# adaLN's sums over partitions on VectorE instead of on TensorE and ScalarE

## The chip, the cores and the metric

The kernel runs on one core of one Trainium2 chip. The metric is the device time of one execution in microseconds (us). The engines are called TensorE (PE in the profile, its weight loads PEld), VectorE (DVE), ScalarE (ACT), GpSimd (POOL) and SyncE (SP, which issues the DMAs).

## The reference

One layer of a conditioned short-convolution mixer on a sequence of 256 positions, all in float32, with D = 2048 and E = 4096:

```python
def rmsnorm(x, g):
    y = xf * lax.rsqrt(jnp.mean(xf * xf, axis=-1, keepdims=True) + EPS)
    return (y * g.astype(jnp.float32)).astype(x.dtype)

def adaln(h, c, w, b):                       # w: (D, 3 D)
    mod = jnp.einsum('bd,df->bf', jax.nn.silu(c), w) + b
    shift, scale, gate = jnp.split(mod, 3, axis=-1)
    h = h * (1.0 + scale[:, None, :]) + shift[:, None, :]
    return h, gate

def short_conv_mixer(h, w_in, conv_w, w_out):
    b_gate, c_gate, v, g = jnp.split(jnp.einsum('bsd,de->bse', h, w_in), 4, axis=-1)
    u = causal_depthwise_conv(c_gate * v, conv_w)
    y = b_gate * u * jax.nn.silu(g)
    return jnp.einsum('bse,ed->bsd', y, w_out)

h, gate = adaln(rmsnorm(x, norm_g), c, ada_w, ada_b)
x = x + gate[:, None, :] * short_conv_mixer(h, sc_w_in, sc_conv_w, sc_w_out)
return rmsnorm(x, final_g)
```

What matters here is `mod`: a vector-matrix product over D = 2048 rows of `ada_w`. Its first 4096 columns give shift and scale, without which `h`, and so the large product with `w_in`, cannot be formed.

## The kernel before, in words

**Products.** Each float32 operand is split into a high part (a cast, `hi`, on ScalarE) and a low part (`lo`, a subtraction on VectorE); a product is three matmuls, hi x hi, hi x lo and lo x hi (`product`, L515). `h` stands transposed as `hT`, 16 k tiles of 128 features; k tile k holds its high part in columns 0 to 255 (written by ScalarE, L361) and its low part behind it (VectorE, L362 and L363).

**The first half of the product with `w_in`** runs while `ada_w` is still being loaded. Output is cut into chunks of 512 columns (chunks 0 to 3, of each of the four quarters c, v, g, b) and each chunk fills one PSUM bank pair (a "bank" below; three of them are used in turn, `mm_s`). The features become ready in eight groups of two k tiles; group 0 (k tiles 0 and 1) is summed in another way before the loop, groups 2, 4, ..., 14 (named by their first k tile) in it. So each (pair of chunks, quarter) is done in several passes over the k tiles that are ready; `plan()` makes the list of 30 passes before anything is emitted. A pass over two chunks with two k tiles is one *block* of 48 matmuls; a longer pass has several. There are 65 blocks, counted from 0. The order is fixed ahead, and each engine executes its instructions in the order in which the program emits them (`in_order`), as long as not all features are ready.

When a pass ends, its banks are closed (`close_bank`, `keep`): in the first pass over an output the bank is copied to SBUF (`acc`, ScalarE, L551). A later pass either adds its bank to `acc` on VectorE (L553), or is *seeded*: ScalarE copies `acc` into the bank before the pass (`open_bank`, L690), the matmuls add to it, and ScalarE copies it out again (L551). `plan()` chooses between the two for each bank by comparing its estimated clocks of ScalarE and VectorE.

**One group of adaLN sums.** Partition p holds the 16 rows p, 128 + p, 256 + p, ... of `ada_w`, so a group's sum over D is a weighted sum over 16 slices, which VectorE makes in 8 pieces of two instructions of 128x512 (`ada_sums`, L495 for the first slice, L497 for the others; columns: shift and scale, two k tiles of 128 each), and a sum over the 128 partitions. For the latter `ada_turn` (L504) has TensorE transpose the four 128x128 parts into a PSUM tile `tp_g`, and `ada_total` (L511) has ScalarE run over each with a copy that accumulates, which gives `gs`, one column of 128 for each part. `all_scales` (L656 to L658, VectorE, three instructions) adds the biases and multiplies by the norm's weight; `all_features` (L361 on ScalarE, L362 and L363 on VectorE, once for each k tile) makes `hT`.

**The emission loop** (L740 to L796) walks through the blocks and keeps a clock for each engine with estimated durations (`SUM_US`, `HI_US`, `TOTAL_US` and so on) to decide what goes where. For block b it emits: the closing of the last pass's second bank; the high part of block b+2; pieces of adaLN sums that end before that high part does (`sum_some`); the low part of block b+2; what is missing of the features that this block needs (`get_ready`); seeds of the next pass; more pieces; the products of the first chunk. Between the products of its two chunks stand the transposes of a group whose pieces ended at least `TURN_US` before that point on the planner's TensorE clock (`turn_sums`), the closing of the pass's first bank and the opening of the next one's second, the totals (`total_sums`), the scales, the features, and again pieces that fit. A piece's DMA is issued when an earlier piece is summed (four are held), the weights of block b+3 when the low part of block b is made.

**Behind this stage** (from about 380 us) the rest of `w_in` (`mm_b`) and `w_out` (`mm_o`) follow; the change doesn't touch them.

Of the kernel before, what the change touches and what calls it, by code (L numbers as in the profile page):

```python
# [8 lines left out]
F32 = mybir.dt.float32  # L9
F32R = mybir.dt.float32r  # L10
AF = mybir.ActivationFunctionType
ALU = mybir.AluOpType

P = 128
# [36 lines left out]
RAW0 = 22.9  # L51
FIRST = 24.0
ISSUE_US = 2.0
TURN_US = 1.0
EARLY_US = 2.0
CONV_AT = 44
LOAD_US = 2.65
# [4 lines left out]
SUM_US = 1.5  # L62
STALL_US = 0.4
AHEAD_US = 3.0
ADD_US = 1.22
COPY_US = 1.03
TOTAL_US = 1.9
FEATURE_US = 0.5


# [4 lines left out]
def plan():  # L75
    steps, ready = [], [0.0] * ADA[0]
    done = {}
    pieces = [(sum(ADA[:g]), nk, i) for g, nk in enumerate(ADA) if g for i in range(4 * nk)]
    load, pe, dve, act = 0.0, 4.0, 0.0, 0.0
    burst = SLOT // P  # L80
    credit = 0.0

    def ada():
        nonlocal load, dve
        piece = pieces.pop(0)
        load = max(load, dve - AAHEAD) + ALOAD
        dve = max(dve, load + 2.0) + VPIECE
        if piece[2] == 4 * piece[1] - 1:
            ready.extend([dve + ALAG] * piece[1])
        return piece  # L90

    def products(n, need):

        nonlocal load, pe, dve, act, credit
        between = []
        load = max(load, pe - WAHEAD)
        pe = max(pe, need, load + min(n, burst) * LOAD + WLAG) + n * PRODUCTS
        for s0 in range(0, n, burst):
            sn = min(burst, n - s0)
            load += sn * LOAD  # L100
            act = max(act, load + 2.0) + sn * SBLOCK
            dve = max(dve, load + 2.0) + sn * VBLOCK
            credit += SHARE * sn / burst
            between.append([])
            while pieces and credit >= 1.0:
                credit -= 1.0
                between[-1].append(ada())
        return between

    order = [((ch, ch + 1), q) for ch in range(0, NCH, 2) for q in QUARTERS]  # L110
    new = [((0,), QUARTERS[0]), ((1,), QUARTERS[0])] + order[1:]
    while new or any(k < KT for k in done.values()):
        before = []
        hi = sum(r <= pe for r in ready)
        if new:
            p = new.pop(0)
            k0 = done[p] = 0
            if p not in order:
                del done[p]
                done[order[0]] = hi  # L120
        else:
            old = [p for p in order if done[p] < KT]
            p = old[0] if hi == KT else min(old, key=lambda p: done[p])
            k0 = done[p]
            while hi == k0:
                while len(ready) == hi:
                    before.append(ada())
                    credit -= 1.0
                pe = max(pe, ready[hi])
                hi = sum(r <= pe for r in ready)  # L130
        between = products((hi - k0) * CT * len(p[0]), ready[hi - 1])
        hows = []
        for _ in p[0]:
            seed = k0 > 0 and act < dve
            if k0 == 0:
                act += SCOPY
            elif seed:
                act += SSEED
            else:
                dve += VSUM  # L140
            hows.append(seed)
        steps.append((before, *p, k0, hi, hows, between))
        if p in order:
            done[p] = hi
    blocks = [b for step in steps for b in step[-1]][: len(PACE)]
    some = [piece for b in blocks for piece in b]
    for b, n in zip(blocks, PACE):
        b[:], some = some[:n], some[n:]
    blocks[-1].extend(some)
    return steps  # L150
# [3 lines left out]
def short_conv_layer(ctx: ExitStack, tc: tile.TileContext, x, c, norm_g, ada_w, ada_b, w_in, conv_w, w_out, final_g, out):  # L154
    nc = tc.nc
# [6 lines left out]
    const = ctx.enter_context(tc.tile_pool(name="const", bufs=1))  # L162
# [3 lines left out]
    psum = ctx.enter_context(tc.tile_pool(name="psum", bufs=3, space=PSUM))  # L166
# [58 lines left out]
    pinned.enter_context(in_order())  # L225


    rows1 = const.tile([80, P], F32, tag="rows1", name="rows1")
    rows2 = const.tile([96, P], F32, tag="rows2", name="rows2")
    HX = D // 2  # L230
    GIVE = 300
# [12 lines left out]
    for n in range(KT // 4):  # L244
        at = wpool.tile([P, SLOT], F32, tag=("lo", "hi")[n % 2], name="at0", bufs=3)
# [50 lines left out]
    b_shift = vec[:, 16:32]  # L296
    b_scale1 = vec[:, 32:48]
    b_both = vec[:, 16:48].rearrange("p (s k) -> p s k", s=2)
    sh_sc = const.tile([P, KT // 2, 2], F32, tag="shsc", name="sh_sc")
    idle(1, turned[2])  # L300
    idle(2, turned[2])
# [194 lines left out]
            else:  # L496
                nc.vector.scalar_tensor_tensor(out=gv, in0=at4[:, i], scalar=c_k, in1=gv, op0=ALU.mult, op1=ALU.add)  # L497

    def ada_turn(k0, nk):

        tp = psum.tile([P, 4, P], F32, tag="sm", name="tp_g", bufs=2)
        gv = sums[k0][:, :, 0 : nk * P]
        for o in range(2 * nk):
            nc.tensor.transpose(tp[:, o, :], gv[:, o // nk, (o % nk) * P : (o % nk + 1) * P], ident)  # L504
        return tp

    def ada_total(nk, tp):

        gs = const.tile([P, 4], F32, tag="gs", name="gs", bufs=2)
        for o in range(2 * nk):  # L510
            nc.scalar.activation(tp[:, o, :], tp[:, o, :], AF.Copy, accum_out=gs[:, o : o + 1])  # L511
        return gs[:, 0:nk], gs[:, nk : 2 * nk]

    opener = [None]
    def product(dst, hi, lo, k, i, begins, left, ends):  # L515
# [45 lines left out]
    N = len(flat)  # L561
    todo = [item for b, block in enumerate(flat) for item in [("w", b)] + [("a", p) for p in block[-1]]][1:]
    raws, parted = {}, {0: (hi0, lo0)}
    waiting, turning, totals, whole_sums, scaled = [], [], [], [], []
    banks = {}
    clock = dict(dma=RAW0, pe=FIRST, dve=RAW0 - ISSUE_US, act=FIRST)
    ready = [NK0]
# [4 lines left out]
    def spend(engine, us, since=0.0):  # L572

        clock[engine] = max(clock[engine], since) + us
        return clock[engine]
# [47 lines left out]
    def sum_one():  # L623

        (k0, nk, piece), at4, at = waiting.pop(0)
        ada_sums(k0, nk, piece, at4)
        spend("dve", SUM_US, at)
        if piece == 4 * nk - 1:
            turning.append((k0, nk, clock["dve"]))
        issue()  # L630

    def sum_some(end, stall):

        while waiting and waiting[0][2] <= clock["dve"] + stall and max(clock["dve"], waiting[0][2]) + SUM_US <= end:
            sum_one()

    def turn_sums(by):

        while turning and turning[0][2] <= by:
            k0, nk, _ = turning.pop(0)  # L640
            totals.append((k0, nk, ada_turn(k0, nk)))

    def total_sums():

        while totals:
            k0, nk, tp = totals.pop(0)
            whole_sums.append((k0, nk, ada_total(nk, tp), spend("act", TOTAL_US, clock["pe"])))

    def all_scales():

        while whole_sums:
            k0, nk, (sums_shift, sums_scale), at = whole_sums.pop(0)
            while waiting and max(clock["dve"], waiting[0][2]) + SUM_US <= at + STALL_US:
                sum_one()
            ks = slice(k0, k0 + nk)
            nc.vector.tensor_tensor(out=scale[:, ks], in0=sums_scale, in1=b_scale1[:, ks], op=ALU.add)  # L656
            nc.vector.tensor_tensor(out=scale[:, ks], in0=scale[:, ks], in1=gT[:, ks], op=ALU.mult)
            nc.vector.tensor_tensor(out=shift[:, ks], in0=sums_shift, in1=b_shift[:, ks], op=ALU.add)  # L658
            spend("dve", STALL_US, at)
            scaled.append((k0, nk))  # L660

    def all_features():
# [9 lines left out]
    def get_ready(k):  # L672

        while ready[0] < k:
            while not turning and not totals and not whole_sums and not scaled:
                issue()
                sum_one()
            turn_sums(clock["dve"])
            total_sums()
            all_scales()  # L680
            all_features()
# [58 lines left out]
    for b, (n, chs, q, k0, k1, seeds, w, s0, sk, _) in enumerate(flat):  # L740
# [20 lines left out]
                open_bank(n + 1, 1)  # L761
        adds = last and len(chs) == 2 and k0 > 0 and not seeds[0]
        sum_some(begin + us / len(chs), STALL_US)
        hi, lo = parted.pop(b)
        parted[b] = None
        for j in range(len(chs)):
            bank = banks[n, j]
            if b == 0:
                for k in range(NK0):
                    chunk_products(bank, hi, lo, k * w, k, k0, k1, late=True)  # L770
            elif k0 == 0 and b + j < 4:
                opening_products(bank, hi, lo, w, j * CT * P, s0, sk, k1)
            else:
                for i in range(sk):
                    chunk_products(bank, hi, lo, i * w + j * CT * P, s0 + i, k0, k1, seeds[j])
            if j == 0:
                clock["pe"] = begin + us / len(chs)
                turn_sums(clock["pe"] - TURN_US)
                if last and len(chs) == 2:
                    close_bank(n, 0)  # L780
                    if n + 1 in passes:
                        open_bank(n + 1, 1)
                total_sums()
                all_scales()
                all_features()
                sum_some(end + AHEAD_US, STALL_US)
                mix_some(end + AHEAD_US)
# [232 lines left out]
```

## Time and profile before

| | |
|---|---|
| Time, median of 3 runs | 913.02 us (911.69 to 913.05) |
| The profiled execution's own time | 911.95 us |
| Its span, first to last instruction | 910.2 us |
| Mean granted TensorE clock | 0.998 |
| TensorE busy | 897.1 us (99%) |
| VectorE busy | 633.5 us (70%) |
| ScalarE busy | 453.1 us (50%) |
| Blocks 0 to 64 (`mm_s`) | about 24 to 379 us |
| Transposes of the sums (L504) | 28, from 61.2 to 239.7 us |
| Their totals on ScalarE (L511) | 28, from 62.8 to 241.2 us |

A page and several views were read. In the groups of instructions a row is "line engine operation out<-in shapes xcount | busy us, mean ns | idle us before them <-what ended it". In the timeline a row is "start us, us, engine line operation out<-in shapes xcount [idle before <-what ended it]"; instructions of one kind that follow each other are merged. In the chain of waits a row is "start us, us, what": the piece of work that the end of the program waited for at that time. The waits view has "who <- for whom: us in total, times, longest us". In the table of windows each engine has its busy us and its count of instructions, then the granted clock, the share of the DMA engines and GB/s. VectorE's and ScalarE's instructions overlap a little at their ends, so the time from one start to the next is often 0.07 to 0.1 us shorter than the duration.

### The profile page before, as it was taken

The numbers are of one execution on the slowest core, as the hardware profiler recorded it, in microseconds if no ns is written. First come the engines' busy times: TensorE is split into PE (matmuls) and PEld (weight loads), VectorE is DVE, ScalarE is ACT, GpSimd is POOL, SyncE is SP. The second block draws the span as 40 slices with busy tenths as digits, with TensorE's granted clock in tenths as the row PEclk, the third lists the DMA queues.
The fourth block names the chain that finished last, engine by engine and source line by source line (L and its number), as shares of the span: only waits on it lengthen the run. The fifth ranks groups of instructions, "written<-read, shape, count | busy, mean of one in ns | idle before, by whom it ended". The sixth has DMA issues, their size and how long they took to land.

```text
span 910.2 us, 16162 instructions
## 1 busy us (share of the span) xinstructions
PE 897.1 (99%) x7045; PEld 859.1 (94%) x7045; DVE 633.5 (70%) x603; ACT 453.1 (50%) x430; POOL 1.8 (0%) x8
## 2 busy tenths in 40 slices
PE   7999999999999999999999999999999999999996
PEld 4999999999999999999999999999999988888885
DVE  5788889999656868776666666656666644555882
ACT  6788766455545746543344443344333433433333
POOL 0000000000000000000000000000000000000000
PEclk9999999999999999999999999999999999999999
DMA  9999999999565555797687778777877496665542
GB/s 310 379 382 364 313 339 347 324 325 354 198 206 190 186 190 201 246 304 240 211 262 245 237 223 269 242 237 230 256 241 240 143 358 205 201 204 188 186 139 92
DMA packets 146855, 227.63 MB, mean 250 GB/s; under 512 B 5456, under 2 KB 103904, under 8 KB 146400
## 3 DMA queue, kind: packets, MB, share of 16 engines
q1 hardware_dynamic: 146688, 226.56, 74.4%
q8 instruction: 55, 0.90, 0.4%
q14 instruction: 16, 0.13, 0.0%
q0 software_dynamic: 64, 0.02, 0.0%
q10 hardware_dynamic: 32, 0.01, 0.0%
HBM read 224.48 MB, written 2.10 MB: 249 GB/s over the span
## 4 chain that ended last, share of the span: by engine, by line
PE 95%; DMA 3%; ACT 1%; DVE 1%; SPq 0%; issue 0%; ACTq 0%
PE mm_b L519 38%; PE mm_s L519 37%; PE mm_o L917 6%; PE mm_o L918 6%; PE mm_o L916 6%; DMA at<-in_ada_w_dram 2%; DMA raw_s<-in_sc_w_in_dram 1%; DMA raw<-in_sc_w_in_dram 0%; PE tp_g L504 0%; ACT hi L611 0%; PE ps_gate L854 0%; SPq L236 0%; ACT tp_g L511 0%; DVE lo L444 0%; DVE lo L618 0%
## 5 line engine op out<-in xcount | busy, mean ns | idle before, releaser
L519 PE MATMUL mm_b<-hT,hi 128*128 128x256 f32 x2048 | 348.4, 276 | 0.0
L519 PE MATMUL mm_s<-hT,hi 128*128 128x256 f32 x2048 | 347.2, 277 | 0.7 <-DVE hT L363 0.5
L519 PEld LDWEIGHTS mm_b<-hT,hi 128*128 128x128 f32 x2048 | 308.6, 188 | 0.1
L519 PEld LDWEIGHTS mm_s<-hT,hi 128*128 128x128 f32 x2048 | 306.5, 188 | 1.5 <-DVE hT L363 0.7
L519 PE MATMUL mm_b<-hT,lo 128*128 128x256 f32 x1024 | 282.6, 276 | 0.0
L519 PE MATMUL mm_s<-hT,lo 128*128 128x256 f32 x1024 | 277.5, 276 | 0.2 <-DVE lo L618 0.2
L370 DVE TENSOR_TENSOR lo<-raw,hi 128x2048 fp32r<-128x2048 f32 x64 | 146.7, 2292 | 114.9 <-ACT hi L369 114.9
L369 ACT CAST hi<-raw 128x2048 fp32r<-128x2048 f32 x64 | 122.5, 1913 | 197.7 <-PE mm_b L519 142.5
L519 PEld LDWEIGHTS mm_b<-hT,lo 128*128 128x128 f32 x1024 | 192.2, 188 | 0.0
L519 PEld LDWEIGHTS mm_s<-hT,lo 128*128 128x128 f32 x1024 | 189.8, 188 | 0.4 <-DVE lo L618 0.4
L618 DVE TENSOR_TENSOR lo<-raw_s,hi 128x2048 fp32r<-128x2048 f32 (+1 forms) x64 | 145.5, 2273 | 49.1 <-ACT hi L611 47.7
L611 ACT CAST hi<-raw_s 128x2048 fp32r<-128x2048 f32 (+1 forms) x64 | 121.5, 1898 | 105.1 <-PE mm_s L519 82.7
L370 DVE TENSOR_TENSOR lo<-raw_o,hi 128x2048 fp32r<-128x2048 f32 x32 | 73.3, 2290 | 63.6 <-ACT hi L369 63.4
L369 ACT CAST hi<-raw_o 128x2048 fp32r<-128x2048 f32 x32 | 61.0, 1907 | 106.4 <-PE mm_o L918 84.5
L917 PE MATMUL mm_o<-lo,y 128*128 128x512 f32 x256 | 99.3, 389 | 0.0
L918 PE MATMUL mm_o<-hi,y 128*128 128x512 f32 x256 | 99.3, 389 | 0.0
L916 PE MATMUL mm_o<-hi,y 128*128 128x512 f32 x256 | 99.3, 389 | 0.0
L497 DVE SCALAR_TENSOR_TENSOR gv<-at,silu_c,gv 128x512 f32<-128x512 f32 x105 | 78.7, 750 | 2.7
L916 PEld LDWEIGHTS mm_o<-hi,y 128*128 128x128 f32 x256 | 48.1, 188 | 10.0
L917 PEld LDWEIGHTS mm_o<-lo,y 128*128 128x128 f32 x256 | 48.0, 188 | 10.0
L918 PEld LDWEIGHTS mm_o<-hi,y 128*128 128x128 f32 x256 | 48.0, 188 | 9.9
L551 ACT COPY acc<-mm_s 128x1024 f32<-128x1024 f32 x43 | 43.2, 1013 | 9.0 <-PE mm_s L519 8.7
(106 smaller groups left out, 377.6 us busy)
## 6 DMA issues: line engine op xcount, KB each, us to landing
raw<-in_sc_w_in_dram SPq DMA_DIRECT2D x64, 1024.0 KB, 6.7
raw_s<-in_sc_w_in_dram SPq DMA_DIRECT2D x63, 1024.0 KB, 6.0
raw_o<-in_sc_w_out_dram SPq DMA_DIRECT2D x32, 1024.0 KB, 5.2
at<-in_ada_w_dram SPq DMA_DIRECT2D x126, 256.0 KB, 6.7
at_g<-in_ada_w_dram SPq DMA_DIRECT2D x32, 512.0 KB, 7.5
x<-in_x_dram SPq DMA_DIRECT2D x4, 512.0 KB, 6.3
big<-in_x_dram SPq DMA_DIRECT2D x2, 1024.0 KB, 7.6
out_dram<-big SPq DMA_DIRECT2D x4, 512.0 KB, 2.9
```

Source lines behind the costliest of these rows:

```text
L369: nc.scalar.copy(hi[:, :n], raw[:, :n])
L370: last_low[0] = nc.vector.tensor_tensor(out=lo[:, :n], in0=raw[:, :n], in1=hi[:, :n].bitcast(F32), op=ALU.subtract)
L497: nc.vector.scalar_tensor_tensor(out=gv, in0=at4[:, i], scalar=c_k, in1=gv, op0=ALU.mult, op1=ALU.add)
L519: mm = last_mm[0] = nc.tensor.matmul(dst, w, h[:, k], start=begins and left, stop=ends, skip_group_check=True)
L551: nc.scalar.copy(acc[ch, q], bank)
L611: nc.scalar.copy(hi[:, :n], raws[b][:, :n])
L618: nc.vector.tensor_tensor(out=lo[:, :n], in0=raws.pop(b)[:, :n], in1=hi[:, :n].bitcast(F32), op=ALU.subtract)
L916: nc.tensor.matmul(po, yh, hi[:, o], start=opens, stop=False, skip_group_check=True)
L917: nc.tensor.matmul(po, yh, lo[:, o], start=False, stop=False, skip_group_check=True)
L918: nc.tensor.matmul(po, yl, hi[:, o], start=False, stop=ct == NCT - 1, skip_group_check=True)
```

## The change

The sum over partitions of a group moves to VectorE. The 128x512 tile of a group is transposed in blocks of 32x32 into a PSUM tile, so that what lay in 32 partitions of one column lies in 32 neighbouring columns of one partition; a sum over those 32 columns leaves 16 columns (`by_block`, 128x16); four copies bring the four groups of 32 partitions next to each other in 32 partitions (`side`); and four small sums over the four groups write `gs`, one for each 32 partitions of the result. Both small tiles lie in columns of `rows1`, a tile whose rows were used up at the start. The transposes on TensorE and the accumulations on ScalarE are gone, and with them `turn_sums`.

The emission changes with it. The totals are emitted in two places: in `get_ready`, and in each block ahead of its first products, behind the low part and the pieces. They wait for no point of the TensorE clock. They spend 2.1 us on the planner's VectorE clock (before: 1.9 on ScalarE's). `all_scales` no longer emits pieces ahead of the scales. In `plan()`, every bank of a later pass over more than two k tiles is seeded, whatever the clocks say.

```diff
-TURN_US = 1.0
...
-TOTAL_US = 1.9
+TOTAL_US = 2.1
...
-            seed = k0 > 0 and act < dve
+            seed = k0 > 0 and (act < dve or hi - k0 > 2)
...
-    rows1 = const.tile([80, P], F32, tag="rows1", name="rows1")
+    rows1 = const.tile([P, P], F32, tag="rows1", name="rows1")
...
+    by_block = rows1[:, 0:16]
+    side = rows1[0:32, 16:80].rearrange("p (g b) -> p g b", g=4)
...
-    def ada_turn(k0, nk):
-
-        tp = psum.tile([P, 4, P], F32, tag="sm", name="tp_g", bufs=2)
-        gv = sums[k0][:, :, 0 : nk * P]
-        for o in range(2 * nk):
-            nc.tensor.transpose(tp[:, o, :], gv[:, o // nk, (o % nk) * P : (o % nk + 1) * P], ident)
-        return tp
-
-    def ada_total(nk, tp):
-
-        gs = const.tile([P, 4], F32, tag="gs", name="gs", bufs=2)
-        for o in range(2 * nk):
-            nc.scalar.activation(tp[:, o, :], tp[:, o, :], AF.Copy, accum_out=gs[:, o : o + 1])
-        return gs[:, 0:nk], gs[:, nk : 2 * nk]
+    def ada_total(k0, nk):
+
+        tp = psum.tile([P, 512], F32, tag="sm", name="tp_g", bufs=2)
+        nc.vector.transpose(tp, sums[k0].rearrange("p s f -> p (s f)"))
+        nc.vector.reduce_sum(by_block, tp.rearrange("p (b j) -> p b j", j=32), axis=mybir.AxisListType.X)
+        for g in range(4):
+            nc.vector.tensor_copy(out=side[:, g, :], in_=by_block[32 * g : 32 * g + 32, :])
+        gs = const.tile([P, 2, nk], F32, tag="gs", name="gs", bufs=2)
+        for g in range(4):
+            nc.vector.reduce_sum(
+                gs[32 * g : 32 * g + 32], side.rearrange("p g (s k b) -> p b s k g", s=2, k=nk)[:, g], axis=mybir.AxisListType.X
+            )
+        return gs[:, 0], gs[:, 1]
...
     def total_sums():
 
-        while totals:
-            k0, nk, tp = totals.pop(0)
-            whole_sums.append((k0, nk, ada_total(nk, tp), spend("act", TOTAL_US, clock["pe"])))
+        while turning:
+            k0, nk = turning.pop(0)
+            whole_sums.append((k0, nk, ada_total(k0, nk)))
+            spend("dve", TOTAL_US)
 
     def all_scales():
 
         while whole_sums:
-            k0, nk, (sums_shift, sums_scale), at = whole_sums.pop(0)
-            while waiting and max(clock["dve"], waiting[0][2]) + SUM_US <= at + STALL_US:
-                sum_one()
+            k0, nk, (sums_shift, sums_scale) = whole_sums.pop(0)
...
-            spend("dve", STALL_US, at)
+            spend("dve", STALL_US)
...
         sum_some(begin + us / len(chs), STALL_US)
+        total_sums()
         hi, lo = parted.pop(b)
...
                 clock["pe"] = begin + us / len(chs)
-                turn_sums(clock["pe"] - TURN_US)
                 if last and len(chs) == 2:
                     close_bank(n, 0)
                     if n + 1 in passes:
                         open_bank(n + 1, 1)
-                total_sums()
                 all_scales()
                 all_features()
```

More of the change, by code (lines that the diff above doesn't have):

```diff
@@ L563, in short_conv_layer @@
     raws, parted = {}, {0: (hi0, lo0)}
-    waiting, turning, totals, whole_sums, scaled = [], [], [], [], []
+    waiting, turning, whole_sums, scaled = [], [], [], []
     banks = {}
@@ L628, in sum_one @@
         if piece == 4 * nk - 1:
-            turning.append((k0, nk, clock["dve"]))
+            turning.append((k0, nk))
         issue()
@@ L635, in sum_some @@
             sum_one()
[L637 to L641, printed above, removed]
     def total_sums():
-        while totals:
-            k0, nk, tp = totals.pop(0)
-            whole_sums.append((k0, nk, ada_total(nk, tp), spend("act", TOTAL_US, clock["pe"])))
+        while turning:
+            k0, nk = turning.pop(0)
+            whole_sums.append((k0, nk, ada_total(k0, nk)))
+            spend("dve", TOTAL_US)
     def all_scales():
         while whole_sums:
-            k0, nk, (sums_shift, sums_scale), at = whole_sums.pop(0)
-            while waiting and max(clock["dve"], waiting[0][2]) + SUM_US <= at + STALL_US:
-                sum_one()
+            k0, nk, (sums_shift, sums_scale) = whole_sums.pop(0)
             ks = slice(k0, k0 + nk)
@@ L674, in get_ready @@
         while ready[0] < k:
-            while not turning and not totals and not whole_sums and not scaled:
+            while not turning and not whole_sums and not scaled:
                 issue()
                 sum_one()
-            turn_sums(clock["dve"])
             total_sums()
```

## The prediction, made before the result was known

> **What bounds the kernel now.** I read the page first: the busy shares and the chain that ended last.
>
> ```profile
> span 910.2 us, 16162 instructions
> PE 897.1 (99%) x7045; PEld 859.1 (94%) x7045; DVE 633.5 (70%) x603; ACT 453.1 (50%) x430; POOL 1.8 (0%) x8
> PE 95%; DMA 3%; ACT 1%; DVE 1%; SPq 0%; issue 0%; ACTq 0%
> ```
>
> TensorE (PE) is the bound: 95% of the chain is its own work. So two things alone can move the end: work that leaves or joins TensorE's queue, and waits that TensorE gains or loses. VectorE (DVE) and ScalarE (ACT) count only where TensorE would wait for them. The waits view says where it waits for the adaLN features now, and the chain in order of time shows that place.
>
> ```profile
> PEld mm_s L519 <- DVE hT L363: 0.7, 1, 0.7
> ...
> 61.43 0.44 PE tp_g L504 x4
> 61.86 32.70 PE mm_s L519 x288
> 94.56 0.45 PE tp_g L504 x4
> ...
> 97.09 0.61 ACT hT L361
> ...
> 98.18 0.44 DVE hT L363
> 98.61 0.04 issue
> 98.66 6.43 PE mm_s L519 x54
> ...
> 239.55 0.44 PE tp_g L504 x4
> ```
>
> There is one such wait in the program, of 0.7 us as the view counts it: block 14 begins, needs the features of k tile 4, and gets them at 98.6. A row below gives it at the matmuls: one starts at 97.75, the next at 98.66, against 32.70 / 288 = 0.1135 us from one to the next elsewhere, so 0.8 us were lost. The seven groups of transposes (L504, the first at 61.43, the last at 239.55) lie on the chain with 0.44 to 0.45 us each.
>
> The stage in which all this happens, 39 to 241 us, has a busy VectorE: 202.00 - 180.57 = 21 us of idle time.
>
> ```profile
> 39.00:241.00 202.00, 201.28 (x1767) 200.81 (x1767) 180.57 (x194) 134.84 (x155) 0.00 (x0) 1.00 0.96 336
> ```
>
> **The change, part by part. What TensorE loses.** Seven times four transposes.
>
> ```profile
> 61.27 0.60 PE L504 MATMUL tp_g<-ident,gv 128*128 128x128 f32 x4
> 61.62 0.48 PE L519 MATMUL mm_s<-hT,hi 128*128 128x256 f32 x2
> 97.75 0.38 PE L519 MATMUL mm_s<-hT,hi 128*128 128x256 f32 x1
> 98.66 0.38 PE L519 MATMUL mm_s<-hT,hi 128*128 128x256 f32 x1 [0.53 <-DVE hT L363]
> ```
>
> On the chain a group is worth 0.44; the pair of matmuls behind it takes 0.48 us where such pairs elsewhere take 0.38 or 0.39, so at most 0.53. I take 0.47: 7 x 0.47 = 3.3 us gained, bounds 3.1 and 3.7.
>
> **What VectorE gets: the length T of one new total.** It is a block transpose of 128x512, a sum over 512 elements, four copies of 32x16 and four sums of 32x16. None of these is in the trace. The nearest rows:
>
> ```profile
> L495 DVE TENSOR_SCALAR gv<-at,silu_c 128x512 f32<-128x512 f32 x7 | 3.4, 479 | 0.0
> L852 DVE TENSOR_TENSOR gate_s<-gacc,gate_s 128x512 fp32r<-128x512 f32 x4 | 2.7, 684 | 0.0
> L497 DVE SCALAR_TENSOR_TENSOR gv<-at,silu_c,gv 128x512 f32<-128x512 f32 x105 | 78.7, 750 | 2.7
> 64.40 0.16 DVE L656 TENSOR_TENSOR scale<-gs,vec 128x2 f32<-128x2 f32 x1
> 64.60 0.16 DVE L657 TENSOR_TENSOR scale<-scale,vec 128x2 f32<-128x2 f32 x1
> 64.68 0.15 DVE L658 TENSOR_TENSOR shift<-gs,vec 128x2 f32<-128x2 f32 x1
> ```
>
> The two large ones: 0.48 to 0.75 each; I take 0.68, the middle row, as for one element after the other. The eight small ones: L658, which needs nothing of L657, begins 0.08 behind it; L657, which needs L656, begins 0.20 behind it. So 0.08 to 0.20 each, I take 0.13. T = 2 x 0.68 + 8 x 0.13 = 2.4 us, bounds 2 x 0.48 + 8 x 0.08 = 1.6 and 2 x 0.75 + 8 x 0.20 = 3.1. (The kernel's new planner constant, 2.1, lies between.) [...]
>
> VectorE loses 12 of its 15 adds of a bank to a kept partial sum (L553). In the plan, worked through with the new condition, no pass moves, but the second bank of every pass of more than two k tiles becomes a seed, which ScalarE copies in (L690) and out (L551).
>
> ```profile
> L551 ACT COPY acc<-mm_s 128x1024 f32<-128x1024 f32 x43 | 43.2, 1013 | 9.0 <-PE mm_s L519 8.7
> L690 ACT COPY mm_s<-acc 128x1024 f32<-128x1024 f32 x27 | 27.3, 1011 | 3.3 <-DVE acc L553 3.1
> L553 DVE TENSOR_TENSOR acc<-mm_s,acc 128x1024 f32<-128x1024 f32 x15 | 18.3, 1220 | 5.1 <-PE mm_s L519 4.9
> L511 ACT ACTIVATE tp_g<-tp_g 128x128 f32<-128x128 f32 x28 | 7.4, 263 | 2.9 <-PE tp_g L504 2.3
> L511 ACT ACTIVATION_READ_ACCUMULATOR tp_g<-tp_g 128x1 f32 x28 | 5.4, 194 | 0.0
> ```
>
> ScalarE loses 7.4 + 5.4 = 13 us and gains 12 x 2.0 = 24, in a stage of which it now works 134.84 of 202 us.
>
> **The first new wait, block 8.** Before, a group's transposes were put behind the TensorE clock of the planner, its totals on ScalarE a block later. Now nothing is asked: the total stands behind the low part that VectorE makes in the same block. Group 2 is whole in block 6, so VectorE does: low part of block 8, total, scales. ScalarE stands in its queue at the features, ahead of the copy that frees the second bank of pass 6, and there waits. That bank is the first of pass 8, block 8.
>
> ```profile
> 57.77 2.29 DVE L618 TENSOR_TENSOR lo<-raw_s,hi 128x2048 fp32r<-128x2048 f32 x1 [0.25 <-ACT hi L611]
> 59.98 0.48 DVE L495 TENSOR_SCALAR gv<-at,silu_c 128x512 f32<-128x512 f32 x1
> 57.64 2.12 ACT L551 COPY acc<-mm_s 128x1024 f32<-128x1024 f32 x2
> 60.07 1.91 ACT L611 CAST hi<-raw_s 128x2048 fp32r<-128x2048 f32 x1 [0.32 <-DVE lo L618]
> 61.89 1.00 ACT L551 COPY acc<-mm_s 128x1024 f32<-128x1024 f32 x1
> 64.86 1.10 ACT L361 ACTIVATE hT<-xs,shift,scale 128x256 fp32r<-128x256 f32 x2 [0.49 <-DVE shift L658]
> 65.87 0.99 ACT L551 COPY acc<-mm_s 128x1024 f32<-128x1024 f32 x1
> ```
>
> VectorE is free for the total at 59.98, where L495 starts now. Then T, 0.46 from the first scale to the features (64.40 to 64.86), 1.01 for ScalarE's two features (to 65.87), 0.99 for the copy: the bank is free at 62.44 + T = 64.84; now its copy (the second of the two at 57.64) is done by 59.8. TensorE gets there at 61.87 + 24 x 0.1135 - 0.47 = 64.12 (half a block behind the transposes, less what they cost). Wait 0.7. Behind that copy stand the high part of block 9 (61.89 - 60.07 = 1.82) and the copy of 1.0 for the next bank, 2.82 against half a block of 2.72: 0.1 more. Together 0.8, in general T - 1.6.
>
> **The second, block 14.** The total also sits in the planner's VectorE clock, which I carried on with the new rules: piece 0 of group 4 no longer fits ahead of the low part of block 9, and the group stays one piece late. Block 11's part of the queue begins with the low part of block 13, which must await the end E of block 10 on TensorE (now the copy at 80.99 starts on it). From there VectorE is never free: low part of 13, two pieces, the add of pass 10 (one of the three that stay), low part of 14, two pieces, low part of 15, total, scales, features.
>
> ```profile
> 80.99 1.02 ACT L551 COPY acc<-mm_s 128x1024 f32<-128x1024 f32 x1 [0.75 <-PE mm_s L519]
> 87.52 1.22 DVE L553 TENSOR_TENSOR acc<-mm_s,acc 128x1024 f32<-128x1024 f32 x1
> 88.65 2.28 DVE L618 TENSOR_TENSOR lo<-raw_s,hi 128x2048 fp32r<-128x2048 f32 x1
> 90.85 1.53 DVE L497 SCALAR_TENSOR_TENSOR gv<-at,silu_c,gv 128x512 f32<-128x512 f32 x2
> 92.30 0.48 DVE L495 TENSOR_SCALAR gv<-at,silu_c 128x512 f32<-128x512 f32 x1
> ```
>
> Start to start: 1.13 for the add, 2.20 for a low part, 1.46 for a piece of two instructions. So E + 1.92 (high part of 13, by the 1.91 at 60.07) + 3 x 2.20 + 4 x 1.46 + 1.13 + T + 0.46 + 1.52 (97.09 to 98.61) = E + 17.5 + T. TensorE asks for the features after three blocks of 48, E + 3 x 5.45 = E + 16.3. Wait 1.2 + T = 3.6, against 0.8 now: 2.8 more. What arrived at E drops out, so block 8's wait doesn't cushion this one. If the weights of block 12, whose load is issued behind the later low part of block 9, also come late, it grows by up to 0.6.
>
> **Behind it** I cost the change at nothing. The other five groups are whole at least two blocks before they are used, and no other wait for features stands in the view of now; VectorE gains 7 x 2.4 = 16.8 and loses, up to 241 us, five adds of 1.22, which is 10.7 of 21 us of idle time. The thinnest are groups 6 and 8: by the queue they are ready some 2 us ahead of their blocks. If that cover is gone, it is one more wait of T less 2.
>
> **Sum**: -3.3 + (T - 1.6) + (T + 1.2 - 0.8) = 2 T - 4.5, which is +0.3 us at T = 2.4, -1.3 at 1.6, +1.7 at 3.1. On the profiled execution of 911.95 (span 910.2) that is 912.25. It lies 1.07 below the median of 913.02 (runs 911.69 to 913.05); on the median the forecast is 913.3. A measurement of this kernel can tell about 0.2%, 1.8 us, from no change.
>
> **The rivals.** *The cover holds* (faster): the totals fit into VectorE's idle time and neither wait comes, block 14's own included: -3.3 - 0.8 = -4.1, 908.9. For it: 21 us of idle time, and the new total needs no turn in the queues of two other engines. Against it: the idle time lies in pieces of 0.2 to 0.8 us ahead of low parts, and both chains above leave out none of it. It needs T below 1.3 or another order than I worked out. Chance 0.14.
>
> *The total is long* (slower): the block transpose streams at half the rate, 1.22 as L553 takes for 1024 elements, and every small instruction waits for the one before: 1.22 + 0.68 + 8 x 0.20 = 3.5. Then 2 x 3.5 - 4.5 = +2.5, 915.5. It decides the sign from T = 3.15. [...] Chance 0.2. [...]
>
> *Seeds come late* (slower): ScalarE's 12 new copies into a bank stand ahead of the second half of a block; if two or three of them are late by their own 1.0 us, the sum is +2.3 to +3.3, 915 to 916. Against it: the seeds that exist make TensorE wait nowhere that the chain shows, and ScalarE has a third of the stage idle. Chance 0.04.
>
> **How the numbers follow.** Forecast (T 1.6 to 3.1): 0.62, from 911.7 to 914.7. The range reaches to 916.0 for the long total and the late weights, and down to 910.8 for a spread of 1.3 between runs and an easier block 8; what it leaves out is most of the first rival and a tail of the second. Faster: 0.14 and nearly nothing of the forecast, 0.15. Slower: 0.2 and 0.04, 0.24. Same: the rest, 0.61.
>
> **What would show it.** Right: no L504 row; TensorE waits for a bank's copy (L551) at about 64 us by 0.7 and for hT at block 14 by 3 to 4 us; one total takes 2.4 us of VectorE; L690 x39 and L553 x3. Wrong: a wait at block 14 below 1 us (the order or T), new waits behind 110 us (the cover), or seeds that TensorE waits for.

## The result and the profile after

The changed kernel takes 915.86 us (median of 6 runs, 915.34 to 917.01), the kernel before 912.70 (6 runs, 911.69 to 913.05): ratio 1.0037, interval 1.0024 to 1.005. It is slower by 0.37%. The time lies in the predicted range, at its upper end (916.0), and 2.6 us above the forecast of 913.3. The forecast held that the change could not be told from no change; it can, and it is slower. The profiled execution after took 916.17 us, 4.2 more than that of before.

First the page of the kernel after: span, busy shares, and the granted clock in 40 slices of 22.9 us.

```profile
span 914.3 us, 16140 instructions
PE 897.6 (98%) x7017; PEld 859.1 (94%) x7017; DVE 638.0 (70%) x661; ACT 465.7 (51%) x398; POOL 1.8 (0%) x8
PEclk9999899999999999999999999999999999999999
```

TensorE has 28 instructions fewer, and its busy time is not smaller but 0.5 us larger. The row of the clock says why: one slice, the fifth (91 to 114 us), holds an 8. Before it held only nines. The stage shows it too, with the busy time and count of PE, PEld, DVE, ACT and POOL and then the clock:

```profile
39.00:241.00 202.00, 196.92 (x1703) 196.14 (x1703) 179.62 (x238) 132.65 (x110) 0.00 (x0) 0.98 0.91 320
```

TensorE is idle for 5.1 us of it (before 0.7), and the clock is 0.98 (before 1.00). VectorE and ScalarE each do slightly less than before in this stage (179.62 us after 180.57, 132.65 after 134.84): the engine that took over the work is not overloaded. The waits of TensorE's weight loads, and the groups of the new work:

```profile
PEld mm_s L519 <- ACT hT L362: 3.6, 1, 3.6
...
PEld mm_s L519 <- ACT acc L551: 1.7, 2, 1.3
...
PEld mm_s L519 <- DVE hT L364: 0.6, 1, 0.6
```

```profile
L551 ACT COPY acc<-mm_s 128x1024 f32<-128x1024 f32 x55 | 55.1, 1012 | 9.6 <-PE mm_s L519 9.6
L682 ACT COPY mm_s<-acc 128x1024 f32<-128x1024 f32 x39 | 39.6, 1016 | 1.9 <-DVE acc L553 1.2
...
L503 DVE STREAM_TRANSPOSE tp_g<-gv 128x512 f32<-128x512 f32 x7 | 5.0, 719 | 0.0
L504 DVE TENSOR_REDUCE rows<-tp_g 128x16 f32<-128x512 f32 x7 | 4.8, 691 | 0.2
L509 DVE TENSOR_REDUCE gs<-rows 32x4 f32<-32x16 f32 x28 | 4.8, 171 | 0.5
L506 DVE COPY rows<-rows 32x16 f32<-32x16 f32 x28 | 4.6, 163 | 0.5
L553 DVE TENSOR_TENSOR acc<-mm_s,acc 128x1024 f32<-128x1024 f32 x3 | 3.7, 1218 | 0.0
```

(Lines have moved: the features on ScalarE are L362 now, those on VectorE L363 and L364, the seeds L682, the scales L649 to L651.) So the predicted waits came, one for a bank's copy (1.3 us; the second of the two, 0.4, stood in the view of before too) and one for the features of one block. The seeds are 39 and the adds 3, as worked out.

**Block 8.** The timeline of the kernel after, VectorE, ScalarE and TensorE:

```profile
57.67 2.29 DVE L618 TENSOR_TENSOR lo<-raw_s,hi 128x2048 fp32r<-128x2048 f32 x1 [0.17 <-ACT hi L611]
59.88 0.72 DVE L503 STREAM_TRANSPOSE tp_g<-gv 128x512 f32<-128x512 f32 x1
60.64 0.69 DVE L504 TENSOR_REDUCE rows<-tp_g 128x16 f32<-128x512 f32 x1
61.36 0.69 DVE L506 COPY rows<-rows 32x16 f32<-32x16 f32 x4
62.09 0.72 DVE L509 TENSOR_REDUCE gs<-rows 32x4 f32<-32x16 f32 x4
62.84 0.16 DVE L649 TENSOR_TENSOR scale<-gs,vec 128x2 f32<-128x2 f32 x1
...
63.31 1.09 ACT L362 ACTIVATE hT<-xs,shift,scale 128x256 fp32r<-128x256 f32 x2 [4.75 <-DVE shift L651]
64.31 0.99 ACT L551 COPY acc<-mm_s 128x1024 f32<-128x1024 f32 x1
...
64.00 0.28 PE L519 MATMUL mm_s<-hT,lo 128*128 128x256 f32 x1
65.35 0.50 PE L519 MATMUL mm_s<-hT,hi 128*128 128x256 f32 x2 [1.07 <-ACT acc L551]
```

The total runs from 59.88 to 62.84: T = 2.96 us. ScalarE stands 4.75 us at the features, its copy of the bank begins at 64.31 instead of 61.89, and TensorE goes from one matmul to the next in 1.35 us instead of 0.1135; with a slow pair behind it 1.35 are lost.

**Block 14.** The chain of waits gives the predicted road: from the end of block 10 on TensorE, where ScalarE begins the high part of block 13, to the features.

```profile
81.93 1.93 ACT hi L611
...
102.65 9.37 PE mm_s L519 x57
```

(The view ends at 112 us, and with it its last row.) From 81.93 to 102.65 are 20.7 us; the prediction had 17.5 + T. At the matmuls:

```profile
98.05 0.28 PE L519 MATMUL mm_s<-hT,lo 128*128 128x256 f32 x1
101.74 0.58 PE L519 MATMUL mm_s<-hT,hi 128*128 128x256 f32 x1 [3.42 <-ACT hT L362]
102.65 0.58 PE L519 MATMUL mm_s<-hT,hi 128*128 128x256 f32 x1 [0.33 <-DVE hT L364]
103.03 0.41 PE L519 MATMUL mm_s<-hT,lo 128*128 128x256 f32 x1
103.24 0.63 PE L519 MATMUL mm_s<-hT,hi 128*128 128x256 f32 x2
```

From 98.05 to 102.65 lie two steps that take 0.23 us in a full stream: 4.4 us lost, before 0.9 (97.49 to 98.66). And then something that no step of the prediction has: the matmuls behind the wait take 0.58 instead of 0.38 us. The windows after, and below them two of the same windows before:

```profile
98.00:102.60 4.60, 0.91 (x4) 0.41 (x3) 3.64 (x16) 1.51 (x3) 0.00 (x0) 0.86 1.02 367
...
104.00:106.00 2.00, 2.00 (x11) 2.00 (x11) 1.99 (x1) 0.88 (x1) 0.00 (x0) 0.50 0.04 12
106.00:108.00 2.00, 2.00 (x12) 2.00 (x11) 1.45 (x3) 0.04 (x1) 0.00 (x0) 0.50 0.38 61
108.00:110.00 2.00, 2.00 (x18) 2.00 (x18) 0.00 (x0) 1.97 (x2) 0.00 (x0) 0.96 0.92 348
110.00:112.00 2.00, 2.00 (x20) 2.00 (x20) 0.00 (x0) 1.21 (x2) 0.00 (x0) 1.00 0.98 351
```

```profile
104.00:106.00 2.00, 2.00 (x20) 2.00 (x19) 1.29 (x2) 1.78 (x1) 0.00 (x0) 1.00 0.91 356
106.00:108.00 2.00, 2.00 (x20) 2.00 (x20) 1.83 (x1) 1.04 (x2) 0.00 (x0) 1.00 0.96 340
```

From 104 to 108 us TensorE is busy throughout and does 11 or 12 matmuls in 2 us where before it did 20. Narrower windows show a granted clock of 0.50 from 101.35 us, still inside the wait, to 108.17. Block 14 lasts 9.15 us from its first matmul to the end of its last. A run below in which the clock holds has 6.53. So the half clock costs 2.6 us in this execution, out of TensorE's busy time, where no list of waits shows it.

The profiled pair: -3.15 for the transposes (seven times 0.45: a step of 0.47 and a slow pair, less two normal steps), +1.35 at block 8, +3.4 of idle time at block 14, +2.6 of half clock: +4.2. The span grew by 4.1.

The theory: the order of VectorE's queue makes the total late in two places, and the longer of the two waits throws TensorE's clock down. The rivals: the seeds, which were changed in the same diff, cost the time; or the total itself, at 2.96, does.

### The profile page after: what moved, and what is told of

Same layout as the page of the kernel before. It is cut to its first block, busy times and chain, and to the rows that moved or that the text cites. A ratio compares the mean times of both kernels' runs of the same rounds, so it can differ in the third digit from the quotient of the medians.

```text
span 914.3 us, 16140 instructions
## 1 busy us (share of the span) xinstructions
PE 897.6 (98%) x7017; PEld 859.1 (94%) x7017; DVE 638.0 (70%) x661; ACT 465.7 (51%) x398; POOL 1.8 (0%) x8
## 4 chain that ended last, share of the span: by engine, by line
PE 90%; DMA 5%; DVE 2%; ACT 1%; issue 1%; ACTq 0%; SPq 0%
PE mm_b L519 38%; PE mm_s L519 32%; PE mm_o L907 6%; PE mm_o L909 6%; PE mm_o L908 6%; DMA raw_s<-in_sc_w_in_dram 3%; DMA at<-in_ada_w_dram 2%; ACT hi L611 1%; DVE lo L618 1%; DMA x<-in_x_dram 1%; DVE gv L498 1%; PE ps_gate L845 0%; DVE rows L504 0%; DVE gs L509 0%; DVE tp_g L503 0%
## 5 line engine op out<-in xcount | busy, mean ns | idle before, releaser
L551 ACT COPY acc<-mm_s 128x1024 f32<-128x1024 f32 x55 | 55.1, 1012 | 9.6 <-PE mm_s L519 9.6
```

The costliest lines, as they stand in the source:

```text
L551: nc.scalar.copy(acc[ch, q], bank)
```

## The experiments

Each ratio is to the kernel before on the same chip. After itself, run again beside `group2`, `group4` and `prompt_old_seeds`, took 915.42 us (1.0034, 1.0022 to 1.0047).

**The clock: `filler`.** 15 matmuls that nobody reads fill the wait at block 14. The features come no earlier.

```diff
+            if b == 14:
+                fill = psum.tile([P, 512], F32, tag="sm", name="fill", bufs=2)
+                for _ in range(15):
+                    nc.tensor.matmul(fill, hT[:, 0, 0:P], hT[:, 0], start=True, stop=True, skip_group_check=True)
```

> The changed kernel with 15 matmuls of 512 columns that nobody reads, put on TensorE just ahead of block 14, where it waits 3.6 us for the features. Clock theory: the 2.6 us that block 14 lost on top of its wait are the half clock that follows an idle TensorE; with the fillers (15 x 0.23 = 3.4 us, inside the wait) the clock stays at 1.0, block 14 takes 5.6 to 6.5 us in place of 9.2, and the kernel is 2 to 2.6 us faster than the changed one (913.3 to 913.9), about +0.6 to +1.2 against before. Rival: the slow matmuls of block 14 have another cause (fresh features, the transfers of that time); then they stay slow, and the time is that of the changed kernel or longer.

914.19 us (913.74 to 914.77), ratio 1.0019 (1.001 to 1.0028). Timeline and windows of this kernel:

```profile
98.25 3.59 PE L760 MATMUL fill<-hT 128*128 128x512 f32 x15
101.83 0.38 PE L519 MATMUL mm_s<-hT,hi 128*128 128x256 f32 x1
```

```profile
102.00:108.50 6.50, 5.97 (x51) 5.78 (x52) 4.85 (x7) 5.23 (x6) 0.00 (x0) 1.00 0.27 80
```

The block's matmuls start at the same point as without the filler (101.83, after 101.74), the clock stays at 1.00, and the kernel is faster although TensorE does more: by 1.7 us from median to median, by 1.4 when each is taken against the kernel before on its own chip (+3.2 and +1.8). That the half clock comes from TensorE's idleness is thereby shown. The gain is less than the 2 to 2.6 us that were expected from the profile of after. Its executions probably don't all lose so much: over its six runs the mean clock lay between 0.994 and 0.997, over the filler's eleven between 0.997 and 0.999.

**The same wait without the change: `before_delay4` and `before_delay7`.** In the kernel before, 4 or 7 adds of 128x512 that change nothing the output uses are put on VectorE ahead of the scales of group 4.

```diff
+            if k0 == 4:
+                for _ in range(4):                       # or 7
+                    nc.vector.tensor_tensor(out=sums[k0], in0=sums[k0], in1=sums[k0], op=ALU.add)
```

> The kernel before, with 4 additions of 128x512 on VectorE that nobody reads, ahead of the scales of group 4 (4 x 0.65 = 2.6 us, of which 0.6 fill a gap). Clock theory: block 14's features are 2.0 us later, TensorE waits 2.1 and then 0.8 us, too short for the clock to fall: +2.0 us against before, clock 1.0 in block 14. Rival (any wait of some us halves the clock): +3 to +4.6.

> The same with 7 additions: 4.55 us, 0.6 of it in the gap, so block 14 waits 4.1 and then 0.8 us, as long as in the changed kernel. Clock theory: half clock behind the wait, 3.9 us for the wait and 1.5 to 2.6 for the clock: +5.4 to +6.5 against before. Rival (the half clock belongs to the changed kernel, not to the wait): +3.9, clock 1.0 in block 14.

915.77 us (1.0032, 1.002 to 1.0044) and 919.11 (1.0067, 1.0054 to 1.0081): +3.2 and +6.5. The waits and a window of the kernel with 4 adds, and a window of that with 7:

```profile
PEld mm_s L519 <- ACT hT L361: 2.2, 1, 2.2
...
PEld mm_s L519 <- DVE hT L363: 0.7, 1, 0.7
```

```profile
100.00:104.00 4.00, 2.77 (x12) 2.58 (x13) 2.63 (x6) 3.79 (x4) 0.00 (x0) 0.70 0.77 300
```

```profile
104.00:108.00 4.00, 4.00 (x28) 4.00 (x28) 3.34 (x4) 2.03 (x3) 0.00 (x0) 0.74 0.00 0
```

The clock falls in a kernel that has nothing of the change. For 7 adds the time came out as the clock theory had it. For 4 adds the theory had a wait too short for that, an estimate of the author's that no run had shown, and it missed: 2.2 and 0.7 us of waiting, with one matmul between, were enough. So far the clock fell with 4.4 us lost (after) and with 2.9 (4 adds); with the 0.9 of before it stayed at 1.00 (97.7 to 112 us).

**The seeds: `seeds_alone` and `seeds_undone`.** The kernel before with the new condition for seeds; the kernel after with the old one.

```diff
-            seed = k0 > 0 and act < dve
+            seed = k0 > 0 and (act < dve or hi - k0 > 2)
```

> The kernel before with only the planner's new seed condition: 12 of 15 adds become copies on ScalarE. My theory: it changes nothing before block 15 and ScalarE has room: within 0.3 us of before, no new wait of TensorE. Rival (the seeds cost the time): +1 to +3 us, with waits of TensorE for a bank's copy.

> The changed kernel with the old seed condition: 15 adds on VectorE again, everything else of the change kept. My theory: both waits lie ahead of the first seed that differs, so blocks 8 and 14 keep theirs and the time is that of the changed kernel within 0.5 us, unless VectorE, with 7 x 3.0 more to do and nothing given back, makes features late at the blocks that had 0.4 to 2 us to spare (k tiles 6, 8, 12): then up to 3 us slower. Rival (the seeds cost the time): 1 to 3 us faster than the changed kernel.

912.88 us (1.0006, 0.9996 to 1.0015) and 924.27 (1.0131, 1.0117 to 1.0145). The seeds by themselves cost nothing that can be told from no change (+0.5 us, where at most 0.3 was expected), and no matmul waits for one; without them the change would have lost 8.4 us more, far more than was expected. The waits and the end of the chain into block 37 of `seeds_undone`:

```profile
PEld mm_s L519 <- ACT hT L362: 8.3, 3, 4.2
```

```profile
228.67 0.61 issue
229.28 2.29 DVE lo L618
231.56 0.65 DVE tp_g L503
...
234.90 0.61 ACT hT L362
```

There are three waits for features instead of one. The last, at 231 us, is block 14's over again: a total behind a low part, TensorE without features, half clock behind it (granted clock 0.86 from 228 to 240 us). VectorE's adds push the whole queue late.

**The length of the total: `one_quadrant`.** All four copies read partitions 0 to 31, so each total takes one group of 32 partitions four times and leaves out the other three; only the time counts.

```diff
-            nc.vector.tensor_copy(out=side[:, g, :], in_=by_block[32 * g : 32 * g + 32, :])
+            nc.vector.tensor_copy(out=side[:, g, :], in_=by_block[0:32, :])
```

> The changed kernel with all four copies of a total reading partitions 0 to 31 (so the sums over partitions are made of one quarter taken four times; time only). If the step to another group of 32 partitions is what makes each small copy wait for the one before, their pitch falls from 0.18 to about 0.08 us, T from 2.96 to about 2.6, block 14's wait by 0.35, and the kernel is 0.7 us faster (twice the difference in T), more if the shorter wait keeps the clock. If 0.18 is simply what such a copy takes, pitch and time stay.

```profile
61.44 0.39 DVE L506 COPY rows<-rows 32x16 f32<-32x16 f32 x4
61.87 0.72 DVE L509 TENSOR_REDUCE gs<-rows 32x4 f32<-32x16 f32 x4
```

Four copies take 0.39 us instead of 0.69, and one starts 0.08 behind the other instead of 0.175: in these copies, stepping through the groups of partitions is what spaces them. The wait at block 14 falls by 0.3 (matmul to matmul 3.39, after 3.69). The time does not show it: 915.95 us (1.0037, 1.0023 to 1.0051), where 0.7 us less than after was expected. That is a miss, and not resolved: its four times spread over 1.8 us, more than 0.3 us at each of two waits.

**The order: `group2`, `group4`, `early`, `prompt`.** `group2` puts the features of group 2 one block later, behind the copy of the bank; `group4` puts total, scales and features of group 4 ahead of the low part of block 15; `early` does both.

```diff
+            if b == 13:                                  # group4, early: between pieces and low part
+                total_sums()
+                all_scales()
+                all_features()
...
-                all_features()
+                if b != 6:                               # group2, early
+                    all_features()
```

> The changed kernel with only the first of the two moves: group 2's features one block later. Theory: block 8's wait of 1.3 us goes; block 14's stays, since it is counted from the end of block 10 and moves with it: 1.3 us faster than the changed kernel. Rival (VectorE is behind anyway, so that the wait only moves to block 14): no faster than the changed kernel.

> The changed kernel with only the second move: group 4's total, scales and features ahead of the low part of block 15. Theory: block 14's wait falls by one low part, 2.2 us, to 2.2 us, under the 3.0 us at which the clock fell in a run so far, so the half clock goes too: 3.5 to 4.5 us faster than the changed kernel, about 912. If the clock falls all the same, 2.2 us faster.

> The changed kernel with two steps moved in the order of emission: the features of group 2 one block later (behind the copy that frees block 8's bank), and total, scales and features of group 4 ahead of the low part of block 15 instead of behind it. Theory (the change loses by where the totals stand in the queues): block 8's wait of 1.3 us goes, block 14 waits about 1.9 us in place of 4.4, the clock stays at 1.0, and the sum is -3.15 for the transposes and +1.1 for block 14: 910.4, 2 us faster than before. Rival (VectorE simply has too much to do, the order is secondary): the waits come back at later blocks and the time stays above 913.

914.41 us (1.0022, 1.0013 to 1.0031), 912.39 (1.0003, 0.9994 to 1.0012) and 911.02 (0.9986, 0.9978 to 0.9995). Against after on the same chip `group2` is worth 1.0 us (1.3 expected) and `group4` 3.0 (2.2 if the clock falls, 3.5 to 4.5 if not), and both together, 4.4 by the ratios to before, come out near the sum. So the loss is the order. At equal waits `early` and `group4` differ in the clock. Both wait at block 14 for the same two lengths, 1.62 and 0.91 us matmul to matmul; two windows, first of `early`, then of `group4`:

```profile
99.00:103.00 4.00, 3.50 (x30) 3.50 (x31) 3.94 (x5) 3.28 (x4) 0.00 (x0) 1.00 0.13 41
103.00:107.00 4.00, 4.00 (x37) 4.00 (x37) 2.78 (x3) 3.43 (x4) 0.00 (x0) 1.00 0.87 294
```

```profile
100.00:104.00 4.00, 3.64 (x21) 3.65 (x22) 3.97 (x5) 2.59 (x2) 0.00 (x0) 0.67 0.03 9
104.00:108.00 4.00, 4.00 (x33) 4.00 (x33) 2.64 (x3) 2.47 (x3) 0.00 (x0) 0.90 0.91 298
```

One holds its clock at 1.00, the other falls. If it falls to 0.50, as in after, the rows 0.67 and 0.90 make about 2.6 and 0.8 us of half clock, 3.4 together; in after it was 6.83 (101.35 to 108.17). So with 2.3 us of waiting the clock fell in one execution and held in another; what decides between the two is not shown. The eleven times of `early` lie in two clusters, 910.2 to 911.0 with mean clocks of 0.997 to 0.999, and 911.9 to 912.6 with 0.995 to 0.997. That the clock fell at block 14 in the slower cluster is likely and not shown, since only one execution of the kernel has a trace (910.54 us, of the faster one).

`prompt` goes one step further: besides `early`, the totals of groups 2 and 4 cost nothing on the planner's clock, so that pieces move forward, and the total of group 4 stands right behind its last piece.

```diff
+            if k0 == 4:                                  # in sum_one, behind the last piece
+                total_sums()
+                all_scales()
...
-            spend("dve", TOTAL_US)
+            spend("dve", TOTAL_US if k0 > 4 else 0.0)
```

> As the last one, and the totals of groups 2 and 4 take no time on the planner's clock, so that the pieces stand as in the kernel before; the total and scales of group 4 come right behind its last piece. Theory: block 14 waits 0.8 to 1.2 us, as before the change; only the 3.15 us of the transposes are left: 909.3, some 3 us faster than before. Rival as above: above 912.

908.73 us (908.59 to 909.33), ratio 0.9958 (0.9945 to 0.997): faster than both kernels. Its timeline:

```profile
92.85 0.73 DVE L503 STREAM_TRANSPOSE tp_g<-gv 128x512 f32<-128x512 f32 x1
...
97.00 0.32 PE L519 MATMUL mm_s<-hT,hi 128*128 128x256 f32 x1
97.85 0.38 PE L519 MATMUL mm_s<-hT,hi 128*128 128x256 f32 x1 [0.53 <-DVE hT L364]
```

The total of group 4 starts at 92.85 instead of 97.67, and of the waits at block 14 0.7 us are left (97.00 to 97.85). The time is 0.6 us below the 909.3 that was expected.

**Seeds once more: `prompt_old_seeds`.** `prompt` with the old condition for seeds.

> The fastest version so far (moved totals) with the planner's old seed condition, 15 adds on VectorE. Theory: VectorE has too little room for 7 totals and 12 adds, so waits for features come at the later blocks 26 and 37, as in the changed kernel with old seeds: 3 to 7 us slower than with the new seeds (912 to 916). Rival (with the order mended the seeds are not needed): within 1 us of 908.7.

909.38 us (0.9964, 0.9951 to 0.9977). The theory from `seeds_undone`, that the seeds carry the change, fell: with the totals in time, undoing them costs 0.7 us, one more wait of 0.8 at 223 us. Here the adds hurt only behind an order that is late already.

## Why the prediction was wrong

**The step that failed is the price of the second wait, "2.8 more".** Place and cause of that wait were right, and its length too once T is put in as measured: 17.5 + T after the end of block 10 (20.5, measured 20.7), with TensorE asking at 16.2 to 16.3. But it was priced as idle time alone. After standing for 4.4 us TensorE did not go on at full speed, and the half clock behind cost 2.6 us in the profiled execution and 1.4 to 1.7 at the median (`filler`). With T as measured the prediction's own sum is 2 x 2.96 - 4.5 = +1.4 us; `filler`, in which the clock holds, measured +1.8. The 1.4 us that are missing to the +3.2 of the medians are the clock. That 915.86 lies in the range is luck: its upper end was put at 916.0 for the long total and late weights, and neither came.

**T was mis-sized**: 2.96 for 2.4. The two large instructions took 0.76 and 0.72 from start to start (0.68 forecast), the eight small ones 1.48 together, 0.185 each (0.13). The prediction had the other end at hand, 0.20 from its own rows, and took the middle. With 0.20 its T would have been 2 x 0.68 + 8 x 0.20 = 2.96. Since T counts twice, the 0.56 us that were missing are +1.1 us, and alone they would have moved 913.3 to 914.4, still within what can't be told from no change.

**The rest held, within tenths.** The transposes are worth 3.15 (3.3 forecast). Block 8 lost 1.35 (T - 1.6 gives the same). "Behind it I cost the change at nothing": no other wait for features stands in the view after. The rival *the total is long* met the time (915.5) by luck: its small instructions did come nearly as slowly as it had them (0.185 each, 0.20 in the rival), but its slow transpose did not come (0.72 us, not 1.22), and T stayed below the 3.15 from which it was to decide. *The cover holds* and *seeds come late* did not occur.

## What to carry to other kernels

A new wait of TensorE can cost more than its length, as in after, `before_delay4`, `before_delay7`, `one_quadrant` and `seeds_undone` (2.9 to 5.1 us of waiting) and in one of two kernels at 2.3: look at the granted clock in the windows behind it, since the loss stands in busy time. Work moved to an engine with idle time is late or not by its place in that engine's queue, not by the share; here the same instructions cost 3.2 us in one order and gain 3.8 in another. When a change brings several parts along, test each in both orders: the seeds were worth 8.4 us in one and 0.7 in the other.

## What the runs showed of the hardware

Half clock lasted 6.83 us in after (101.35 to 108.17, 4.4 us lost) and about 3.4 us in five other profiles, an estimate from the granted clock of windows, with 0.50 taken for the lower clock as in after: `before_delay4` (2.9 us of waiting by the waits of the weight loads; 0.70 and 0.87 from 100 to 104 and 108 us), `before_delay7` (5.1; 0.89 from 98 to 104, 0.74 to 108), `one_quadrant` (4.0; 0.84 and 0.59 from 100 to 103 and 106), `seeds_undone` (4.9 at 231 us; 0.86 from 228 to 240) and `group4` (2.2; 0.67 and 0.90 from 100 to 104 and 108). With the same 2.2 us in `early` and 0.9 lost in before the clock stayed at 1.00. The single matmul inside the wait of `group4` (at 99.45 us) did not prevent the fall; the 15 that filled the wait in `filler` did (1.00 from 98.5 to 108.5). VectorE's 32x32 block transpose of 128x512 float32 from SBUF into PSUM took 0.72 us, a sum over its 512 elements 0.69; elementwise instructions of that size with two tensor operands took 0.68 (L852 of the kernel before) and 0.75 (L497). Copies of 32x16 that step through groups of partitions followed each other at 0.175 us (after), those that read the same group at 0.08 (`one_quadrant`).
